# Opening an encoder trunk in two column halves instead of one pass over all columns

## The chip, the core and the metric

The kernel runs on one core of a Trainium2 chip. It is one launch, and its time is the device time of that launch in microseconds (us). The version before took 1982.92 us in the median of three runs (1982.06 to 1983.12). Five engines work side by side, each in the order of its own queue: TensorE (PE) multiplies matrices, VectorE (DVE) and ScalarE (ACT) work element by element, GpSimd (POOL) does a few odd jobs, and SyncE (SP) issues the transfers between HBM and SBUF. A matrix product needs its left operand in the array first; the profile lists this weight load as PEld.

## The reference

Two layers of an encoder are computed on a sequence of 1024 tokens with 1024 channels. This case is about how the first layer begins:

```python
cond = jax.nn.silu(c)                                  # c: (1, 1024)
mod = cond @ ada_w[0] + ada_b[0]                       # ada_w[0]: (1024, 3072)
shift, scale, gate = jnp.split(mod[:, None, :], 3, axis=-1)
h = rmsnorm(x, norm_w[0]) * (1 + scale) + shift
...
proj = h @ w_in                                        # w_in: (1024, 6176)
qkv, z, b, a = jnp.split(proj, [...], axis=-1)         # b and a: 16 columns each
qkv = jax.nn.silu(causal_depthwise_conv(qkv, conv_w))
...
beta = jax.nn.sigmoid(b)
g = -jnp.exp(A_log) * jax.nn.softplus(a + dt_bias)     # per token and head
o = gated_delta_rule(q, k, v, g, beta)                 # cumulative sums of g, a triangular solve
...                                                    # per chunk, a chain of states over chunks
```

Shift and scale are two vectors of 1024 numbers, each a product of the vector `cond` with 4 MB of weights. Nothing of `h` can be computed before they are there. The gates `b` and `a` are 32 more columns of the same projection, and everything behind them (the decay `exp(g)` between tokens of a chunk, the triangular solve, the chain of states) needs them. The second layer is softmax attention with a forget gate; then a final norm follows.

## The kernel before, in words

The first layer works on two halves of 512 tokens. In each it goes through eight groups of heads; a group needs one tile of keys (k), one of queries (q), two of values (v) and two of the output gate (z). A tile is a product of 128 output columns with 512 tokens over eight blocks of 128 channels. Each block takes three matmuls, because the float32 operands are split into a high and a low part (`ht_h`, `ht_l` for the modulated input, `whi`, `wlo` for the weights): high by high, low by high, high by low (`mm3`, line 337). A tile is thus 24 matmuls of 128x512, here called products.

**What sets the order.** The order on TensorE is written by a planner, the class `Flow` (lines 108 to 183). It adds up an assumed cost of each matmul (lines 121 to 128) and switches between generators: a generator that yields a number is left alone until that much assumed time has passed. The projections (`proj_all`, line 802) are the filler of lowest rank, and the gates, the preparation of a group (`prepk`, `prepv`), the triangular solve (`invert_blocks`, `invert_merge`) and the chain of states (`chain`) are put between them at the due times of the constants at the top (`Y_GA`, `LAT` and so on). On the other engines and on SP's queue a list scheduler of the framework sets the order. No engine runs an instruction ahead of one that stands before it in its queue, apart from weight loads on TensorE.

**The opening** (`start_norm`, line 550). Four tiles of x are loaded, normed and transposed into eight blocks `xsT` (tiles named `k`, `q`, `ktok`, 128 channels x 512 tokens each). Shift and scale then come one after the other, each over all 1024 columns (loop of line 570, n = 0 and 1): eight loads of 512 KB, of which VectorE sums the first seven into `acc` (a tile `d2`, lines 577 and 579; `KPE` = 7), and TensorE adds up the 128 rows of `acc` and of the eighth load by matmuls with one column (`ones`, `cond`, line 584). VectorE adds the bias (line 596: `scol` is the shift, `gcol` the scale). Then all eight blocks are modulated: ScalarE writes `ht_h` (line 605) and, for odd blocks, the unrounded value (line 607); VectorE does that for even blocks (line 609) and subtracts for `ht_l` (line 615). The products for the gates take the modulated block as the left operand and 32 columns `wba` as the right one, in unsplit float32 (line 611: 8 blocks x 4 = 32 matmuls of 128x32). Only then the projections begin.

**The gates** (`gates`, line 703). A row of small VectorE operations on 128x64 turns the products into log decays (lines 707 to 718, `g_tmp`), then comes `yield Y_GA` (14000), the cumulative sums on TensorE (lines 722 and 723), four transposes (line 739), a copy by ScalarE (`rows`, line 741), a store to DRAM (`g_d`, line 745), and only with `g_d` there may a group be prepared (line 850). `decay` (line 878) reads two rows of `g_d` back, broadcast to all partitions (`gb`, one buffer), masks them on GpSimd (line 886) and takes eight exponentials on ScalarE (line 897). In `prepk` the keys are transposed, squared and summed on ScalarE (line 943, `sqt`) and copied (line 947); in `prepv` the values are transposed on TensorE (`tr<-ident,vt`) into the two banks `tr`.

**Where the filler ends.** `vt`, the buffer of the value tiles, exists once: the values of group 1 are not projected before those of group 0 are transposed (line 826). So there are 144 products (k, q, v, v of group 0, k and q of group 1) that can run ahead of the gates, and no more.

The next half's x is read early by `next_norm` (line 646): after the gates' cumulative sums two tiles `nx` are loaded, squared by ScalarE (`nh`, line 310) and normed.

## Time and profile before

| | |
|---|---|
| median of three runs | 1982.92 us (1982.06 to 1983.12) |
| the profiled execution | 1981.06 us, its span 1979.3 us, mean granted TensorE clock 0.966 |
| busy share of the span | PE 93%, DVE 67%, ACT 52%, POOL 19% |
| read from HBM, written | 223.15 MB, 81.67 MB |

The profile names an instruction by its line, its engine and the tiles that it writes and reads (`mm<-ht_h,whi`). Times in a timeline row are the start in us from the span's start and the duration; `x3` says that three like instructions are merged in the row; square brackets name idle time of the engine ahead of the row and what ended it. A float32 matmul that isn't split counts as two records. Busy time of TensorE hides its clock: the granted clock has a column of its own.

### The profile page before, as it was taken

What the parts mean: (1) busy time and instruction counts of PE and PEld (TensorE: products, weight loads), DVE (VectorE), ACT (ScalarE), POOL (GpSimd) and SP (SyncE); (2) the same over time, 40 slices, a digit from 0 to 9 for tenths busy, and PEclk for the clock granted to TensorE, in tenths of its full rate; (3) what the DMA queues carried; (4) which work ended last, traced back from release to release, by engine and by line L of the source; (5) the groups of instructions that cost most, each with busy time, mean ns of one, the idle gap of its engine ahead of it and who ended that gap; (6) DMA issues with size and microseconds to landing.
All of it is one profiled execution on the core that took longest, in us unless ns stands there. A gap on an engine that the chain in (4) does not pass through costs nothing.

```text
span 1979.3 us, 35876 instructions
## 1 busy us (share of the span) xinstructions
PE 1838.8 (93%) x12892; PEld 1536.0 (78%) x12892; DVE 1334.9 (67%) x3321; ACT 1030.6 (52%) x2672; POOL 375.2 (19%) x402
## 2 busy tenths in 40 slices
PE   4989989999898999999999889999999999999898
PEld 4868777777786777787777667788988889889676
DVE  6577877888776777776655676456656656656764
ACT  4455656665554445555544444256556655655631
POOL 2010101111111010100010243332232232231322
PEclk6889999999998999999999999999999999999999
DMA  7477556766665564554389985021111120211523
GB/s 265 165 232 245 182 179 198 251 219 225 206 194 170 166 198 146 181 170 137 96 291 311 349 311 201 13 64 49 44 60 38 49 65 27 59 54 49 166 90 96
DMA packets 222874, 307.18 MB, mean 155 GB/s; under 512 B 100396, under 2 KB 136876, under 8 KB 222696
## 3 DMA queue, kind: packets, MB, share of 16 engines
q1 hardware_dynamic: 222696, 304.88, 47.2%
q8 instruction: 102, 1.67, 0.3%
q14 instruction: 76, 0.62, 0.1%
HBM read 223.15 MB, written 81.67 MB: 154 GB/s over the span
## 4 chain that ended last, share of the span: by engine, by line
PE 60%; DVE 15%; DMA 14%; ACT 4%; issue 3%; SPq 3%; POOL 2%; DVEq 0%; POOLq 0%; ACTq 0%
PE mm L132 38%; PE lg L132 5%; PE oT L132 3%; PE pt L136 3%; DMA nx<-in_ada_w_dram 3%; PE su L132 3%; PE tr L136 3%; PE ch L132 2%; DVE wlo L331 2%; DMA lb<-d 1%; PE co L132 1%; DMA lr<-lb 1%; DMA ohi<-og_d 1%; DVE cv_y L792 1%; DVE d L929 1%
## 5 line engine op out<-in xcount | busy, mean ns | idle before, releaser
L132 PE MATMUL mm<-ht_h,whi 128*128 128x512 f32 x768 | 346.2, 451 | 0.2 <-ACT cv_y L784 0.2
L132 PE MATMUL mm<-ht_l,whi 128*128 128x512 f32 x768 | 308.3, 401 | 0.9 <-POOL ht_l L331 0.8
L132 PE MATMUL mm<-ht_h,wlo 128*128 128x512 f32 x768 | 308.6, 402 | 0.0
L132 PE MATMUL mm<-whi,h_h 128*128 128x384 f32 x512 | 186.3, 364 | 0.9 <-DVE kn L1487 0.9
L132 PEld LDWEIGHTS mm<-ht_h,wlo 128*128 128x128 f32 x768 | 148.8, 194 | 34.5
L132 PE MATMUL mm<-whi,h_l 128*128 128x384 f32 x512 | 172.4, 337 | 0.0
L132 PEld LDWEIGHTS mm<-ht_h,whi 128*128 128x128 f32 x768 | 149.9, 195 | 28.6 <-issue 1.7
L132 PE MATMUL mm<-wlo,h_h 128*128 128x384 f32 x512 | 172.1, 336 | 0.0
L132 PEld LDWEIGHTS mm<-ht_l,whi 128*128 128x128 f32 x768 | 149.9, 195 | 26.6 <-POOL ht_l L331 2.0
L1638 DVE TENSOR_TENSOR ptl<-pt,pth 128x512 fp32r<-128x512 f32 x192 | 106.3, 555 | 91.5 <-ACT pth L1637 89.6
L1637 ACT CAST pth<-pt 128x512 fp32r<-128x512 f32 x192 | 91.1, 476 | 138.8 <-PE pt L136 138.0
L792 DVE SCALAR_TENSOR_TENSOR cv_y<-cv_t,conv_h,cv_y 128x512 f32<-128x512 f32 x192 | 143.1, 745 | 16.6 <-ACT cv_y L784 14.4
L331 DVE TENSOR_TENSOR wlo<-ht_h,whi 128x512 fp32r<-128x512 f32 x124 | 97.5, 826 | 47.0 <-ACT whi L328 45.4
L1602 ACT ACTIVATE lg<-lg,mx 128x896 f32<-128x896 f32 (+7 forms) x128 | 99.5, 777 | 53.1 <-DVE mx L1594 47.3
L1481 POOL TENSOR_TENSOR rs<-ss,mhalf 128x4 f32<-128x4 f32 x64 | 64.5, 1007 | 330.6 <-DVE ss L1479 326.2
L328 ACT CAST whi<-ht_h 128x512 fp32r<-128x512 f32 x124 | 70.7, 618 | 89.8 <-DMA ht_h<-in_wa_o_dram 40.1
L132 PE MATMUL mm<-h_h,whi 128*128 128x512 f32 x240 | 99.9, 416 | 0.7 <-DVE wlo L1737 0.3
L132 PEld LDWEIGHTS mm<-whi,h_h 128*128 128x128 f32 x512 | 97.3, 190 | 3.5 <-ACT v L1483 1.2
L132 PEld LDWEIGHTS mm<-wlo,h_h 128*128 128x128 f32 x512 | 96.8, 189 | 2.0
L136 PE MATMUL pt<-ident,lg 128*128 128x128 f32 (+1 forms) x584 | 95.6, 272 | 2.2 <-ACT lg L1602 2.2
L132 PEld LDWEIGHTS mm<-whi,h_l 128*128 128x128 f32 x512 | 96.1, 188 | 0.0
L132 PE MATMUL mm<-h_h,wlo 128*128 128x512 f32 x240 | 94.3, 393 | 0.0
(373 smaller groups left out, 4505.0 us busy)
## 6 DMA issues: line engine op xcount, KB each, us to landing
ht_h<-in_wa_o_dram SPq DMA_DIRECT2D x62, 512.0 KB, 5.6
wc<-whi SPq DMA_DIRECT2D x45, 512.0 KB, 4.3
wc<-wlo SPq DMA_DIRECT2D x45, 512.0 KB, 4.8
wlo<-wc SPq DMA_DIRECT2D x45, 512.0 KB, 4.4
whi<-wc SPq DMA_DIRECT2D x45, 512.0 KB, 3.9
wlo<-in_wa_c_dram SPq DMA_DIRECT2D x35, 512.0 KB, 4.2
nx<-in_ada_w_dram SPq DMA_DIRECT2D x64, 256.0 KB, 4.8
wraw<-in_wb_dram SPq DMA_DIRECT2D x56, 256.0 KB, 2.7
```

The costliest lines, as they stand in the source:

```text
L132: self.nc.tensor.matmul(out, lhsT, rhs, start=start, stop=stop)
L136: self.nc.tensor.transpose(out, src, ident)
L328: nc.scalar.copy(hi, src)
L331: (lo_eng or nc.gpsimd).tensor_tensor(lo, src, hi.bitcast(F32), op=ALU.subtract)
L792: nc.vector.scalar_tensor_tensor(y, raw[:, j : j + HALF], w[:, j : j + 1], y, op0=ALU.mult, op1=ALU.add)
L929: nc.vector.scalar_tensor_tensor(lm[:, u], mq[:, c * P : (c + 1) * P], wn[:, c, j : j + 1], t["d2"][:, u], op0=ALU.mult, op1=ALU.mult,)
L1481: nc.gpsimd.tensor_tensor(rs, ss, mhalf[:, 0:4], op=ALU.pow)
L1602: nc.scalar.activation(lg, lg, AF.Exp, scale=-1.0, bias=mx[:, hh : hh + 1], accum_out=sums[:, tt : tt + 1],)
L1637: nc.scalar.copy(ph_[:, cs], pp[:, cs])
L1638: nc.vector.tensor_tensor(pl_[:, cs], pp[:, cs], ph_[:, cs].bitcast(F32), op=ALU.subtract)
```

## The change

- Shift and scale are no longer computed one after the other over all columns, but together, first for columns 0 to 511 and then for 512 to 1023 (`ada_load`, `ada_sum`). A load is still 512 KB, but each of its rows is now two runs of 2 KB from two places, where it was one run of 4 KB. The small tensors `bcol`, `norm_c`, `wba` and the first weights stand between the two halves, and the sums go to a bank `su`.
- After the first half the blocks 0 to 3 are modulated, and three tiles (`NPRE`, the first three of `proj_all`) begin with their products of those four blocks, in banks `mm`, `mm` and `co`. The first tile goes on with blocks 4 to 7 after the second half, the second with two of them; `proj_tile` finishes the tiles from the list `pre`.
- The gates are now a product with `wba`, split into high and low, as the left operand and 512 tokens as the right one (`gate_mm`, 3 matmuls of 32x512 per block, 24 in all). ScalarE copies the result, four transposes bring it into the form that it had before.
- `Y_GA0` (9000) takes the place of `Y_GA` (14000) for the first half's gates, `LAT0` (33000) that of `LAT` (40000) for the triangular solves of its groups 0 and 1. Both are due times of the planner. Two other lines keep a solve's wait for its banks from being starved (`kept`).

```diff
@@ start_norm: shift and scale @@
-            for n in range(2):
-                ps = banks[n]
-                acc = at([P, D], "d2", 3)
+            def ada_load(c0):
+                acc = at([P, 2, HALF], "d2", 3)
+                ws = []
                 for k in range(KT):
-                    w = at([P, D], *wtag())
-                    nc.sync.dma_start(w, ada_w[0, k * P : (k + 1) * P, n * D : n * D + D])
+                    w = at([P, 2, HALF], *wtag())
+                    nc.sync.dma_start(
+                        w, ada_w[0, k * P : (k + 1) * P, 0 : 2 * D].rearrange("p (n f) -> p n f", n=2)[
+                            :, :, c0 * HALF : c0 * HALF + HALF
+                        ],
+                    )
...
+            def ada_sum(c0, ws):
+                ps = yield from pst("su", 2)
+                for i, (w, c) in enumerate(ws):
+                    for j in range(KT):
+                        n, jj = divmod(j, 4)
+                        mm(
+                            ps[:, j : j + 1], w[:, n, jj * P : (jj + 1) * P], c,
+                            start=i == 0 and j == 0, stop=i == len(ws) - 1 and j == KT - 1,
+                        )
+                cs = slice(4 * c0, 4 * c0 + 4)
+                nc.vector.tensor_tensor(gcol[0][:, cs], ps[:, 4:8], bcol[:, 1, cs], op=ALU.add)
...
@@ start_norm: modulation, gates and first products @@
-                for t in range(CPH):
-                    mm(
-                        pc[:, t * 32 : t * 32 + 32], xk[:, t * P : (t + 1) * P], wba[:, k],
-                        start=k == 0 and t == 0, stop=k == KT - 1 and t == CPH - 1,
-                    )
...
+            split(wbh, wbl, wba, lo_eng=nc.vector)
+            for _ in range(NPRE):
+                wload()
+            half(2 * NPRE)
+            yield from ada_sum(0, ws)
+            ws = ada_load(1)
...
+            def gate_mm(k):
+                mm3(pc[0:32], wbh[:, k], wbl[:, k], ht_h[:, k], ht_l[:, k], k == 0, k == KT - 1)
+
+            def pre_mm(i, k):
+                hi, lo, _ = pws[i]
+                mm3(banks[i], hi[:, k], lo[:, k], ht_h[:, k], ht_l[:, k], k == 0, k == KT - 1)
+
+            for k in range(KT):
+                if k == 4:
+                    yield from ada_sum(1, ws)
+                modulate(k)
+                if k < 4:
+                    for i in range(NPRE):
+                        pre_mm(i, k)
+                    gate_mm(k)
+                else:
+                    gate_mm(k)
+                    pre_mm(0, k)
+            rows = at([P, HALF + 3], "cv_t", 2)[0:32, 0:HALF]
+            nc.scalar.copy(rows, pc[0:32])
...
+            pre_mm(1, 4)
+            pre_mm(1, 5)
...
+                tr_(pg[:, t * 32 : t * 32 + 32], rows[:, t * P : (t + 1) * P], ident[0:32, 0:32])
...
-            yield Y_GA
+            yield (Y_GA0, Y_GA)[h]
...
-            t["end"] = max(flow.t + Y_R2, t0 + LAT)
+            t["end"] = max(flow.t + Y_R2, t0 + (LAT if t["h"] or t["g"] > 1 else LAT0))
```

What this does to the queues is shown at three places. First TensorE, from the sums of shift and scale on. Before, both sums (`mm_267`, `mm_268`, the second in two rows) come first, then the gates, then the first tile:

```order
L132 MATMUL mm_267<-ones_69,d2_270 128x1 x8
L132 MATMUL mm_267<-cond_84,og_292 128x1 x8
L132 MATMUL mm_268<-ones_69,d2_328 128x1 x8
L132 MATMUL mm_268<-cond_84,zg_350 128x1 x8
L132 MATMUL tr_370<-wba_114,k_151 128x32 x4
L132 MATMUL tr_370<-wba_114,k_152 128x32 x4
```

After the first sum the changed kernel has the products of block 0 of three tiles (`mm_368`, `mm_369`, `co_370`), then those of the gates (`tr_367`; `vn` are the halves of `wba`):

```order
L136 MATMUL su_323<-cond_84,og_292 128x1 x8
L136 MATMUL mm_368<-ht_h_149,whi_299 128x512
L136 MATMUL mm_368<-ht_l_150,whi_299 128x512
L136 MATMUL mm_368<-ht_h_149,wlo_301 128x512
L136 MATMUL mm_369<-ht_h_149,whi_307 128x512
L136 MATMUL mm_369<-ht_l_150,whi_307 128x512
L136 MATMUL mm_369<-ht_h_149,wlo_309 128x512
L136 MATMUL co_370<-ht_h_149,whi_315 128x512
L136 MATMUL co_370<-ht_l_150,whi_315 128x512
L136 MATMUL co_370<-ht_h_149,wlo_317 128x512
L136 MATMUL tr_367<-ht_h_149,vn_268 32x512
```

The twelve matmuls of a block repeat for blocks 1 to 3, and only behind these 48 stands the second sum, `su_431`. Then follow three matmuls of the gates and three of the first tile for each of the blocks 4 to 7, six of the second tile, and the four transposes. Ahead of the gates' cumulative sums stand 96 products (before: 69), and ahead of the transposes of group 0's values 144 in both. The solves of groups 0 and 1 stand behind 270 and 339 products (before: 300 and 369); from group 2 to group 6 they stand within 12 products of their old places, later within 36.

Second VectorE, between the two sums. Before, the adds of the second one (`d2_328`, line 579) stand together, with a weight tile's split ahead of the last:

```order
L579 SCALAR_TENSOR_TENSOR d2_328<-og_335,cond_84,d2_328 128x1024
L579 SCALAR_TENSOR_TENSOR d2_328<-zg_338,cond_84,d2_328 128x1024
L579 SCALAR_TENSOR_TENSOR d2_328<-gb_341,cond_84,d2_328 128x1024
L579 SCALAR_TENSOR_TENSOR d2_328<-d1_344,cond_84,d2_328 128x1024
L331 TENSOR_TENSOR wlo_325<-wlo_324,whi_323 128x512 x2
L579 SCALAR_TENSOR_TENSOR d2_328<-og_347,cond_84,d2_328 128x1024
```

In the changed kernel the same adds (`d2_343`, line 591) have the modulation of blocks 0 to 3 between them (lines 622 and 623), and the splits of the second and third weights (`wlo_309`, `wlo_317`) stand behind most of them:

```order
L591 SCALAR_TENSOR_TENSOR d2_343<-zg_353,cond_84,d2_343 128x1024
L623 TENSOR_TENSOR ht_l_150<-k_151,ht_h_149 128x512
L622 TENSOR_SCALAR k_153<-k_153,gcol0_88,scol0_90 128x512
L591 SCALAR_TENSOR_TENSOR d2_343<-gb_356,cond_84,d2_343 128x1024
L623 TENSOR_TENSOR ht_l_150<-k_152,ht_h_149 128x512
L623 TENSOR_TENSOR ht_l_150<-k_153,ht_h_149 128x512
L623 TENSOR_TENSOR ht_l_150<-q_154,ht_h_149 128x512
L591 SCALAR_TENSOR_TENSOR d2_343<-d1_359,cond_84,d2_343 128x1024
L339 TENSOR_TENSOR wlo_309<-wlo_308,whi_307 128x512 x2
L591 SCALAR_TENSOR_TENSOR d2_343<-og_362,cond_84,d2_343 128x1024
L339 TENSOR_TENSOR wlo_317<-wlo_316,whi_315 128x512 x2
```

Between the first sum's columns and the first half of `wlo_317` VectorE has five adds, two modulations, four subtractions and three half splits.

Third VectorE at the gates. Before, the operations on `g_tmp` stand together, and the convolution of the first tile (`cv_y`) follows them:

```order
L323 SCALAR_TENSOR_TENSOR g_tmp<-g_tmp 128x64 x6
L324 SCALAR_TENSOR_TENSOR g_tmp<-g_tmp 128x64
L717 SCALAR_TENSOR_TENSOR g_tmp<-g_tmp 128x64
L718 TENSOR_TENSOR g_tmp<-g_tmp,neg_a 128x64
L331 TENSOR_TENSOR wlo<-wlo,whi 128x512 x2
L792 SCALAR_TENSOR_TENSOR cv_y<-cv_t,conv_h,cv_y 128x512 x3
L799 SCALAR_TENSOR_TENSOR k<-cv_t,cv_y 128x512
```

In the changed kernel they are spread between the convolutions of the first four tiles; these are the last rows of that stretch:

```order
L855 SCALAR_TENSOR_TENSOR cv_y_649<-cv_t_648,conv_h_110,cv_y_649 128x512
L331 SCALAR_TENSOR_TENSOR g_tmp_530<-g_tmp_530 128x64
L332 SCALAR_TENSOR_TENSOR g_tmp_530<-g_tmp_530 128x64
L774 SCALAR_TENSOR_TENSOR g_tmp_530<-g_tmp_530 128x64
L862 SCALAR_TENSOR_TENSOR vt_579<-cv_t_648,cv_y_649 128x512
L775 TENSOR_TENSOR g_tmp_530<-g_tmp_530,neg_a_113 128x64
L782 COPY g_gc_662<-tr_659 128x128
```

From the first operation of the gates (line 764) to the last (line 775), with which the cumulative sums can start, VectorE now has 12 convolution steps, 4 closing products of a tile (line 862), 6 half splits of weights and the gates' own operations. On ScalarE two rows change place: the copy of the gates' rows (line 798) stands behind the squares of `nx` (line 318), which need that tile's load, and the last of the four squares and the copy of group 0's keys stand behind the exponentials of the second group's decay (`d2_843`).

75 lines of the change are left out of this document (47 added, 28 removed).

## The prediction

> **What bounds the kernel now.** I read the busy times by stretches first (columns: busy us and records of PE, PEld, DVE, ACT, POOL; then the granted TensorE clock, DMA share, GB/s).
>
> ```profile
> 40.00:60.00 20.00, 14.90 (x70) 14.68 (x70) 8.06 (x14) 8.57 (x12) 0.00 (x0) 0.50 0.00 0
> 60.00:80.00 20.00, 20.00 (x79) 16.72 (x79) 11.93 (x29) 5.69 (x12) 0.72 (x3) 0.81 0.38 134
> 100.00:120.00 20.00, 14.11 (x70) 11.90 (x69) 11.55 (x36) 14.80 (x52) 5.36 (x7) 0.83 0.72 227
> 220.00:240.00 20.00, 16.40 (x93) 14.28 (x92) 19.61 (x60) 13.19 (x44) 3.96 (x5) 0.87 0.61 211
> 240.00:260.00 20.00, 14.41 (x103) 11.76 (x105) 15.38 (x67) 10.12 (x32) 1.30 (x2) 0.93 0.50 120
> ```
>
> TensorE is the bound nearly everywhere, but not at the start: until 60 us its clock is at half and it does nothing of the projections; between 100 and 120 it idles for 6 us. The timeline of the opening shows why.
>
> ```profile
> 27.68 0.17 DVE L596 TENSOR_TENSOR scol<-mm,bcol 128x8 f32<-128x8 f32 x1 [0.38 <-PE mm L132]
> 43.34 0.17 DVE L596 TENSOR_TENSOR gcol<-mm,bcol 128x8 f32<-128x8 f32 x1 [5.23 <-PE mm L132]
> 43.81 2.22 ACT L605 ACTIVATE ht_h<-k,scol,gcol 128x512 fp32r<-128x512 f32 x3 [6.50 <-DVE gcol L598]
> 50.32 3.63 PE L132 MATMUL tr<-wba,k 128*128 128x32 f32 x16 [3.15 <-ACT k L607]
> 62.29 0.77 PE L132 MATMUL mm<-ht_h,whi 128*128 128x512 f32 x1
> 62.51 0.23 DVE L707 TENSOR_TENSOR g_tmp<-tr,dt_b 128x64 f32<-128x64 f32 x1 [9.41 <-PE tr L132]
> 67.31 0.23 DVE L718 TENSOR_TENSOR g_tmp<-g_tmp,neg_a 128x64 f32<-128x64 f32 x1
> 67.53 0.39 PE L132 MATMUL mm<-ht_h,whi 128*128 128x512 f32 x1
> 80.46 0.33 PE L132 MATMUL tr<-g_tmp,triu 128*128 128x64 f32 x2
> ```
>
> The shift is there at 27.68, the scale at 43.34; then the gates' products run until 62.29, and there both the projections and the gates' operations begin. The 12 products up to 67.53 take 0.44 us each, the 57 up to 80.46 take 0.227: the clock comes up only under them. What limits the next 45 us is the last fence of this part, the way from the gates' cumulative sums (80.46) to the values' transposes.
>
> ```profile
> 82.36 0.24 DVE L654 COPY nx<-g_ngc 128x8 f32<-128x8 f32 x2
> 84.96 1.28 SPq L745 DMA_DIRECT2D g_d<-cv_t  x1
> 100.92 1.10 POOL L886 TENSOR_SCALAR_AFFINE_SELECT d<-gb 128x1024 f32<-128x1024 f32 x1 [2.92 <-PE su L132]
> 102.05 2.44 ACT L897 ACTIVATE d<-d,g_ngc 128x128 f32<-128x128 f32 x8 [2.10 <-POOL d L886]
> 107.61 1.11 PE L136 MATMUL tr<-ident,vt 128*128 128x128 f32 x4 [5.89 <-ACT vtok L964]
> 108.38 0.78 PE L132 MATMUL mm<-ht_h,whi 128*128 128x512 f32 x1
> 111.92 0.40 PE L132 MATMUL mm<-ht_h,wlo 128*128 128x512 f32 x1
> ```
>
> By 102 TensorE has done all 144 products that may run ahead of the gates; it waits 5.89 us and resumes at 108.38, at half clock until 111.92. So what counts is when this chain ends, and not how many of the 144 products were done early: **resume at 108.38** is the mark against which I set the change. From it on both kernels have the same work left.
>
> **The change, step by step** (on the clock of the profiled execution). The prices:
>
> ```profile
> 29.07 1.28 DVE L579 SCALAR_TENSOR_TENSOR d<-zg,cond,d 128x1024 f32<-128x1024 f32 x1
> 36.82 1.29 DVE L331 TENSOR_TENSOR wlo<-wlo,whi 128x512 fp32r<-128x512 f32 x2 [0.56 <-ACT whi L328]
> 44.65 0.55 DVE L609 TENSOR_SCALAR k<-k,gcol,scol 128x512 f32<-128x512 f32 x1 [0.94 <-ACT ht_h L605]
> 45.23 0.69 DVE L615 TENSOR_TENSOR ht_l<-k,ht_h 128x512 fp32r<-128x512 f32 x1
> 49.46 0.80 ACT L607 ACTIVATE k<-k,scol,gcol 128x512 f32<-128x512 f32 x1
> 526.97 0.95 PE L132 MATMUL mm<-ones,nh 128*128 128x1 f32 x8
> 5.00:19.00 14.00, 7.70 (x32) 5.98 (x32) 10.09 (x14) 10.68 (x41) 6.07 (x11) 1.00 1.03 401
> 1000.00:1020.00 20.00, 17.05 (x90) 13.08 (x89) 9.32 (x18) 8.83 (x21) 0.00 (x0) 1.00 1.02 365
> ```
>
> 1. *First columns.* The adds and the sum of the first half are as many as before, so they end as at 27.68. Three small operations in place of one cost 0.4 us. The loads now run in pieces of 2 KB. With rows of 4 KB the engines moved 401 GB/s, in the output projection, with rows of 1 KB among them, 365 at the same share: at most 10% of eight loads of 1.3 us, 1.0 us. I take 0.4, the middle being nearer to 4 KB. The Trainium skill (DMA: Bandwidth & Descriptors, Specifications) states that a transfer of 512 B or more runs at line rate. By it the term is zero and the sum 0.4 us lower; no run here shows pieces of 2 KB alone. Columns at 28.6.
>
> 2. *VectorE up to the third weight.* Five adds (1.3), two modulations (0.55), four subtractions (0.69), three half splits (0.65) are 6.5 + 1.1 + 2.8 + 2.0 = 12.3 us in one queue: 40.9. Until then TensorE has 9 of its 48 products, since `wlo_309` and `wlo_317` are split behind the adds. The adds themselves end at 40 (before: 36.3), hidden under the products.
>
> 3. *The other 39 of the 48*: 12 at 0.44, then 27 at 0.227, 11.4 us: 52.3. All at full clock it would be 8.9, all at half 17.
>
> 4. *Second sum.* 32 records; 43.34 less the 36.3 at which the adds ended, 7.0 us, at half clock, 0.1 us each at full clock (the row at 526.97): 3.2 to 7.0. I take 3.5, since 28 products just ran: 55.8. Here is the price of the new order: the second sum was done at 43.3.
>
> 5. *Second half.* Columns 0.5 us; four `ht_h` at 0.71, one unrounded block 0.8, one subtraction 0.69 until block 5 is there: 60.7. TensorE has six products meanwhile and cools down. Then 17 products: 8 at half clock in 3.5 us, as from 108.38 to 111.92, and 9 at 0.227: 66.2. Six more, 1.4, and four transposes, 0.6, stand ahead of VectorE's first operation on the gates: **68.2, where it was 62.51**. The 12 us of float32 gate products (50.32 to 62.29) are gone, but 54 products and a late second half stand in their place. The row of 111.92 is what the Trainium skill says (TensorE: Matmul & The Clock Gate, The HAM clock gate): an idle window of about 3.4 us halves the clock, a busy one restores it. By it the first heating of step 3 would be 3.4 us too, and the sum 0.8 us lower; the rows at 62.29 and 67.53 show 5.2.
>
> 6. *The gates' operations.* The rows for these:
>
> ```profile
> 72.48 2.33 DVE L792 SCALAR_TENSOR_TENSOR cv_y<-cv_t,conv_h,cv_y 128x512 f32<-128x512 f32 x3 [0.30 <-ACT cv_y L784]
> 75.56 0.69 DVE L799 SCALAR_TENSOR_TENSOR k<-cv_t,cv_y 128x512 f32<-128x512 f32 x1 [0.76 <-ACT cv_t L796]
> ```
>
> They took 5.0 us in one piece (62.51 to 67.54). Now 12 convolution steps (0.78, 9.3 us), four closing products (2.8) and six half splits (3.9) stand among them in the same queue: 21.0 us, ending at 89.2. The 42 products that TensorE has ahead of the cumulative sums are through at 77.7, so it waits 11 us there. **Cumulative sums at 89.2, before 80.46: 8.7 later.**
>
> 7. *From there to the resume* it was 27.9 us. The row copy now waits for `nx`.
>
> ```profile
> 1.23 1.37 SPq L555 DMA_DIRECT2D vtok<-in_x_dram  x3
> 5.10 1.06 ACT L310 ACTIVATE nx<-vtok 128x1024 f32<-128x1024 f32 x1 [2.48 <-DMA vtok<-in_x_dram]
> 98.05 0.58 ACT L947 COPY ktok<-tr 128x512 f32<-128x512 f32 x1
> 102.05 0.32 SPq L881 DMA_DIRECT2D gb<-g_d  x1
> 107.08 1.09 POOL L886 TENSOR_SCALAR_AFFINE_SELECT d<-gb 128x1024 f32<-128x1024 f32 x1
> lb<-d SPq DMA_DIRECT2D x8, 32.0 KB, 2.3
> ```
>
> With nothing queued ahead 512 KB took 3.9 us (1.23 to 5.10) and its squares 1.25: with 1.9 for the copies at 82.36, the copy starts 7.1 us after the sums, not 3.9: +3.2. `g_d` and `gb` took 16.0 together (84.96 to 100.92), with weights and x queued ahead; now little is: 2.3 for the store (as `lb`, the same size) and 5.0 for the read (102.05 to 107.08): -8.6. From the mask to the resume it was 7.5. Now the keys' last square and copy stand behind the second group's exponentials: mask 1.1, second read 5.0, mask 1.1, exponentials 2.4, square and copy 1.0, a tanh and four squares 2.4, transposes 0.8, 13.8: +6.3. Net +0.9, between -3.5 (each transfer a third shorter) and +5 (reads at 7 us).
>
> Resume at 89.2 + 27.9 + 0.9 = 118.0: **9.6 us later.**
>
> 8. *Behind it.* The solves of groups 0 and 1 stand 30 products (6.8 us) nearer.
>
> ```profile
> L1148 DVE STREAM_TRANSPOSE tmat<-rmat x8: 432/436/441, 143.4 to 169.1; 32x256 f32<-32x256 f32 x8
> L132 PE MATMUL su<-tmat,d x160: 177/191/267, 157.5 to 200.9; 16*32 16x16 f32 x64, 32*32 32x32 f32 x64, 64*64 64x64 f32 x32
> ```
>
> The first solve's input was ready at about 145 and used at 157.5: 12 us to spare, which cover the 6.8. I take nothing for it, with 0 to 4 us if the input comes later too. From group 2 on the order is nearly the old one and TensorE the bound, so what is lost at the mark stays lost.
>
> The sum is 1981.06 + 9.6 = 1990.7 us for an execution like the profiled one. That one is 1.9 below the median of the three runs, so I predict **1992.5**. Its own range, from the ends above (gates' start 66 to 71, their stretch 20.4 to 23, step 7 24.5 to 32; not all at once), is 1986 to 1999.
>
> **Rivals.**
> - *The head start pays.* At 67.6 the changed kernel has 54 products done, the one before had them at 67.53 + 42 x 0.227 = 77.1: 9.5 us. If the gates' chain were not what TensorE waits for, all of it would stay: 1973.4. For it speaks that TensorE is busy all through 60 to 100, against it the 5.89 us wait at 107.61. It decides if VectorE reaches the end of the gates' stretch by 71, 18 us sooner than I have it. Chance 0.11.
> - *Short ends, and chains that start sooner.* All of steps 3 to 7 at their short ends put the resume at 109.6, 1.2 later; and the waits of 220 to 260, 9.2 us of idle TensorE by the rows above, go, because the first chains of states stand 30 products further ahead of the filler: 1982.9 + 1.2 - 9.2 = 1974.9. Chance 0.15.
> - *Given back.* The mark is 9.6 late, but those 9.2 us go: 1983.3. VectorE at 19.61 of 20 between 220 and 240 speaks against, since its work is the same. Chance 0.11.
> - *Worse.* TensorE is at half clock through steps 3 and 4 (+8.5) or the solves wait (+4): +14 to +18, 1997 to 2001. Chance 0.18.
>
> That the change does not do what it says is excluded by its order. My forecast keeps 0.45.
>
> **The numbers.** A difference of 0.2%, 4 us, is about what can be told from no change here. Slower by more: forecast, *worse* and a bit of *given back*, 0.64; within: 0.10; faster: 0.26. The range 1975 to 2001 leaves out the first rival, the lower part of the second and the upper end of *worse*, 0.2 in all.
>
> **What would show it.** Right: the second sum's matmuls begin past 50; the gates' first VectorE operation past 66; the cumulative sums with an idle TensorE of about 10 us ahead of them, near 89; the first product behind the values' transposes near 118. Wrong: a resume before 108, or a resume near 118 with an unchanged end.

## The result, and the profile after

| | before | changed |
|---|---|---|
| median | 1983.02 us (4 runs, 1982.06 to 1985.96) | 2013.78 us (4 runs, 2010.19 to 2020.31) |
| ratio, 95% interval | | 1.0162, 1.014 to 1.0185 |
| the profiled execution | 1981.06 us, span 1979.3 us | 2010.19 us, span 2008.0 us |
| mean granted TensorE clock | 0.966 | 0.963 |
| busy share of PE, DVE, ACT, POOL | 93%, 67%, 52%, 19% | 92%, 66%, 51%, 18% |

The change costs 31 us, three times what was forecast, and beyond the upper end of the range. The opening itself went nearly as worked out. These are the rows of the changed kernel's timeline that answer to the steps (start, duration, engine, line, what; in square brackets the idle time ahead and what ended it):

```profile
24.59 3.58 PE L136 MATMUL su<-cond,og 128*128 128x1 f32 x16 [0.58 <-DMA og<-in_ada_w_dram]
29.13 0.15 DVE L608 TENSOR_TENSOR gcol<-su,bcol 128x4 f32<-128x4 f32 x1
40.64 0.79 PE L136 MATMUL co<-ht_h,wlo 128*128 128x512 f32 x1 [0.31 <-DVE wlo L339]
...
52.01 1.84 PE L136 MATMUL su<-ones,d 128*128 128x1 f32 x16
55.81 0.16 DVE L608 TENSOR_TENSOR gcol<-su,bcol 128x4 f32<-128x4 f32 x1 [14.62 <-PE su L136]
67.38 0.22 DVE L764 TENSOR_TENSOR g_tmp<-tr,dt_b 128x64 f32<-128x64 f32 x1
85.71 0.22 DVE L775 TENSOR_TENSOR g_tmp<-g_tmp,neg_a 128x64 f32<-128x64 f32 x1
86.08 0.66 PE L136 MATMUL tr<-g_tmp,triu 128*128 128x64 f32 x2 [8.98 <-POOL cv_t L850]
...
100.16 1.10 POOL L949 TENSOR_SCALAR_AFFINE_SELECT d<-gb 128x1024 f32<-128x1024 f32 x1 [4.02 <-DMA gb<-g_d]
110.13 0.57 ACT L1010 COPY ktok<-tr 128x512 f32<-128x512 f32 x1
110.75 1.11 PE L140 MATMUL tr<-ident,vt 128*128 128x128 f32 x4 [8.32 <-ACT ktok L1010]
112.73 1.12 PE L140 MATMUL tr<-ident,vt 128*128 128x128 f32 x4 [0.87 <-ACT sqt L1006]
```

The second sum begins at 52.01, the gates' row on VectorE at 67.38 and ends at 85.93; TensorE stands idle for 8.98 us ahead of the cumulative sums, and the products resume at about 113.5 us, where it was 108.38. That is 5 us late, not 9.6. So 24 of the 29 us by which the two profiled executions differ are lost behind the mark, where the prediction had put nothing.

To see where, I put a price on each matmul of both traces (the median time to the next matmul, where that one had not waited), summed the prices from the end backwards, and asked for each kernel at what time it has the same TensorE work left as the kernel before. The differences in us, positive when later (the columns behind the first are experiments told below; each is one profiled execution, which can lie 5 us off the median of its kernel, as in runs 7 and 16):

```
time in the  changed  old due  due times prefetch both    one piece  opening,   gates   one tile
kernel before         times    alone     as bef.  undone  in changed one piece  first   deeper
                      (2)      (3)       (5)      (7)     (18)       (14)       (15)    (17)
 120           +5.0    +1.7     -0.8      +6.1     +4.2    -2.7       -9.0       -8.7    -2.0
 220           +5.1    +2.7     -1.9      +5.0     +4.4    -6.9       -7.7       -7.8    -1.1
 280           -4.3    +3.2     -7.2      +0.8     -1.3   -11.4       -6.2       -6.2    -1.1
 520           -0.4    -3.1    -10.9      +2.1     +2.4    -6.3       -6.3       -5.4    -1.5
 560          +11.5    +5.1     -8.8      +3.0     +3.4    +4.8       -5.2       -0.2    +6.9
1000           +8.5    +9.4     -4.9      +6.6     +1.2    +4.9       -0.5      +13.3    +7.5
1100          +13.2    +8.3     -5.1      +9.4     +1.9   +10.6       -0.2      +11.4    +8.5
1200          +23.1    +6.3     +9.8     +24.7     +2.5   +19.2       -3.0      +10.0   +10.5
1960          +28.7    +8.7    +11.1     +26.5    +10.4   +21.3       -0.7      +13.5   +12.3
```

The changed kernel is 5 us late at the mark, *ahead* by 4 us at 280, level at 520, and then loses 12 us at 520 to 560 and 10 us between 1100 and 1200. Of the rest, 3 us come back between 560 and 1000, 5 are lost between 1000 and 1100, and some 5 in small pieces behind 1200.

The gain at 220 to 280 is seen in the busy times by stretch (columns as in the prediction): TensorE is busy for 36.2 of 40 us, before for 30.8.

```profile
220.00:240.00 20.00, 20.00 (x118) 17.49 (x117) 19.52 (x62) 13.23 (x42) 4.96 (x6) 1.00 0.58 200
240.00:260.00 20.00, 16.20 (x196) 12.78 (x195) 17.24 (x52) 10.74 (x34) 0.47 (x2) 0.91 0.87 266
...
530.00:550.00 20.00, 11.63 (x166) 8.48 (x164) 10.24 (x15) 9.01 (x23) 4.44 (x4) 0.74 0.54 161
```

The last row is the first loss: 11.63 us of TensorE in 20, at a granted clock of 0.74. There the second half of the tokens begins. Its normed input is read back from DRAM (`wlo<-h_d`, line 753), ScalarE rounds it to `ht_h`, and the products go on. The timeline of the changed kernel there, from SP's queue to TensorE:

```profile
526.96 9.52 SPq L278 DMA_DIRECT2D nx<-in_ada_w_dram  x5
536.53 0.44 SPq L753 DMA_DIRECT2D wlo<-h_d  x1
...
540.96 1.14 ACT L336 CAST ht_h<-wlo 128x512 fp32r<-128x512 f32 x2 [3.91 <-DMA wlo<-h_d]
...
541.63 0.79 PE L136 MATMUL mm<-ht_h,whi 128*128 128x512 f32 x1 [7.55 <-ACT ht_h L336]
```

And in the kernel before, where the same product starts at 530.63 without a wait:

```profile
530.00:550.00 20.00, 18.29 (x234) 13.71 (x233) 17.08 (x30) 12.97 (x36) 5.97 (x7) 1.00 0.83 282
...
525.38 0.91 SPq L696 DMA_DIRECT2D wlo<-h_d  x2
...
529.11 1.14 ACT L328 CAST ht_h<-wlo 128x512 fp32r<-128x512 f32 x2 [2.63 <-DMA wlo<-h_d]
```

The read is 11 us later, so TensorE waits 7.55 us. The second loss lies in the output projection, which reads `ohi`, `olo` and weights at a DMA share of 0.8 to 1.0. The end of its first half in the changed kernel:

```profile
1125.88 0.42 SPq L1389 DMA_DIRECT2D v<-x_d  x1
1126.35 0.42 SPq L342 DMA_DIRECT2D kn<-in_wb_dram  x1
1127.31 0.32 SPq L1389 DMA_DIRECT2D v<-x_d  x1
1127.67 0.96 SPq L342 DMA_DIRECT2D kn<-in_wb_dram  x1
1128.73 0.59 SPq L443 DMA_DIRECT2D ohi<-og_d  x1
...
1135.56 0.77 PE L136 MATMUL mm<-whi,ohi 128*128 128x512 f32 x1 [4.82 <-DMA ohi<-og_d]
```

and in the kernel before:

```profile
1113.41 0.32 SPq L435 DMA_DIRECT2D ohi<-og_d  x1
...
1114.77 0.32 SPq L1326 DMA_DIRECT2D v<-x_d  x1
1115.14 0.42 SPq L334 DMA_DIRECT2D kn<-in_wb_dram  x1
...
1122.83 0.77 PE L132 MATMUL mm<-whi,yh 128*128 128x512 f32 x1 [3.11 <-DMA yh<-og_d]
```

Four loads of layer 2 (twice 512 KB, twice 256 KB) stand ahead of the last `ohi`, before they stood behind it. The stretch in the changed kernel, with its GB/s in the last column:

```profile
1120.00:1140.00 20.00, 12.45 (x44) 8.29 (x42) 5.55 (x12) 7.03 (x14) 4.77 (x5) 0.85 0.94 324
```

1.5 MB at 324 GB/s would take 4.7 us (an estimate from this row), and TensorE waits 4.82. But the kernel before waits 3.11 us at its next load, `yh`, so these two waits don't make up the 10 us; what the order of these loads costs is left to runs 6 to 8. From its first to its last product, taken from the trace, the whole projection lasts 249.7 us, before 236.0.

### The profile page after: what moved, and what is told of

Its sections match the earlier page's. It is cut to its first block, busy times and chain, and to the rows that moved or that the text cites. A ratio compares the mean times of both kernels' runs of the same rounds, so it can differ in the third digit from the quotient of the medians.

```text
span 2008.0 us, 35824 instructions
## 1 busy us (share of the span) xinstructions
PE 1839.9 (92%) x12856; PEld 1527.5 (76%) x12856; DVE 1331.4 (66%) x3325; ACT 1033.7 (51%) x2674; POOL 365.0 (18%) x402
## 4 chain that ended last, share of the span: by engine, by line
PE 58%; DMA 17%; DVE 14%; ACT 4%; issue 3%; SPq 3%; POOL 1%; DVEq 0%; POOLq 0%; ACTq 0%
PE mm L136 36%; PE lg L136 5%; DMA nx<-in_ada_w_dram 3%; PE pt L140 3%; PE oT L136 3%; PE su L136 3%; PE ch L136 3%; PE tr L140 2%; DMA ohi<-og_d 2%; DVE wlo L339 2%; PE co L136 2%; DVE cv_y L855 1%; DMA ht_h<-in_wa_o_dram 1%; DMA lr<-lb 1%; DMA wraw<-in_wb_dram 1%
## 5 line engine op out<-in xcount | busy, mean ns | idle before, releaser
L136 PEld LDWEIGHTS mm<-ht_l,whi 128*128 128x128 f32 x760 | 148.3, 195 | 28.2 <-DVE ht_l L623 2.3
L339 DVE TENSOR_TENSOR wlo<-ht_h,whi 128x512 fp32r<-128x512 f32 x122 | 91.1, 783 | 53.3 <-ACT whi L336 49.1
```

Source lines behind the costliest of these rows:

```text
L136: self.nc.tensor.matmul(out, lhsT, rhs, start=start, stop=stop)
L339: (lo_eng or nc.gpsimd).tensor_tensor(lo, src, hi.bitcast(F32), op=ALU.subtract)
```

## The experiments

Times are medians in us, ratios against the kernel before on the same chip with their 95% intervals (the changed kernel: 1.0162). Where one differs from its neighbour by less than about 0.3% it tells little: the intervals are that wide.

**1. The reads ahead of the modulation loads.** The first theory was SP's order, in which eight of those loads stand right ahead of the read. Here they must wait for the first read's tile (`where["hf"]`).

```diff
@@ ada_all @@
-            for l, cl in strips:
+            for m, (l, cl) in enumerate(strips):
+                if m == 3:
+                    yield from hold(lambda: "hf" in where)
+                    for _ in range(2):
+                        nc.vector.tensor_copy(al([P, KT], "nx", 2), where["hf"])
```

> The changed kernel, with one edit far from the opening: the loads of layer 2's modulation weights (`nx<-in_ada_w_dram`) from the 25th on may only be issued once the first read of the second half's input (`wlo<-h_d`) has landed. In SP's queue of the changed kernel 34 of them stand ahead of those reads, in the kernel before 26, here 24. *Theory A (two far queues)*: the opening itself costs 5 us at the resume of the products and has given them back by 255 us; the 29 us arise from SP's order at 522 to 536 us (20 us) and from VectorE's order at 1204 to 1221 us (12 us). Then this edit takes 14 to 20 us off, 1994 to 2000; the VectorE order at the second place stands like that of the kernel before here too, and if that counts the time is 1982 to 1988. *Rival B (carried loss)*: what the opening lost is only waited out at 541 us, and would be waited out at the next place otherwise: 2008 to 2016.

Measured: 2015.28, ratio 1.0157 (1.0133 to 1.018). Theory A fell. The modulation loads were gone from there, and still:

```profile
535.87 2.11 SPq L753 DMA_DIRECT2D wlo<-h_d  x2
...
539.46 1.14 ACT L336 CAST ht_h<-wlo 128x512 fp32r<-128x512 f32 x2 [1.72 <-DMA wlo<-h_d]
...
540.13 0.80 PE L136 MATMUL mm<-ht_h,whi 128*128 128x512 f32 x1 [4.30 <-ACT ht_h L336]
```

The read is now issued at 535.87 because a product ended at 535.85, the first half's last: it waited for its buffer `wlo`. The order of the queue was a symptom.

**2. Opening alone, planner as before.**

```diff
-Y_GA0 = 9000
-LAT0 = 33000
+Y_GA0 = 14000
+LAT0 = 40000
@@ Flow.bank @@
-        while key in self.kept:
-            yield 150
```

> The changed kernel with the planner as before: Y_GA0 = 14000, LAT0 = 40000 and without the two lines of `kept`; the opening in two halves alone. Its SP queue has 27 of the loads ahead of the second half's reads (before 26, changed 34). *Theory A*: the far loss at 522 to 557 us is gone, the opening's few us stay: 1980 to 1995. *Rival B (carried loss)*: the opening is what costs, so about the changed kernel's time or more, since the later due times hold the gates back too: 2008 to 2020. *Rival C (the due times cost)*: the new due times are badly set and are the loss, so 1975 to 1985 here.

Measured: 1993.23, ratio 1.0053 (1.0031 to 1.0074), by A's number; but A's reason had fallen, so it says only that opening and due times each do harm.

**3. Due times alone, opening as before.** The three edits of the planner in the old kernel.

> The kernel before with only the planner's part of the change: Y_GA0 = 9000, LAT0 = 33000, `kept`. The opening is the old one. 28 loads stand ahead of the second half's first read and 33 ahead of the last (before 26 and 28). *Theory A*: no loss of its own, 1978 to 1992. *Rival C (the due times cost)*: 2000 to 2012. *Rival B*: as before, 1981 to 1986.

Measured: 1995.09, ratio 1.0062 (1.004 to 1.0085), between A and C. The trace shows more than the time: it is 11 us ahead at 520, and loses 15 us between 1100 and 1200 (third column above), where the changed kernel loses 10. Its projection takes 249.0 us; with the old due times (run 2) it takes 232.9.

**4. The second norm raised in priority.**

```diff
-            scaled(xt, n2jk[t])
+            with tc.high_priority(offset=1000):
+                scaled(xt, n2jk[t])
```

> The changed kernel with the small operations of the second norm (sum, reciprocal root, scaling of `v`) of the last four token tiles raised in the scheduler's priority. In VectorE's queue the scaling of the second tile comes two operations sooner, and the transposed blocks of the next one follow it directly. Nothing is changed at 522 to 557 us. *Theory A*: of the 12 us lost at 1204 to 1221 us some part returns, 2002 to 2012. *Rival B*: no difference, 2011 to 2016.

Measured: 2014.23, ratio 1.014 (1.0097 to 1.0184): no difference to be told, and its projection takes 249.2 us. Raising these operations returns nothing of the 13.7 us by which the projection is longer.

**5. One weight tile less ahead.** In the changed kernel the three tiles begun early each issue a new weight load, so the line of loaded weights is longer by one tile from then on. A tile takes two of the five `wlo` buffers, in a ring, and the reads of `h_d` use the same ring.

```diff
@@ proj_tile @@
                 (hi, lo, key), ps, k0 = pre.pop(0)
-                wload()
+                if len(pre) < NPRE - 1:
+                    wload()
```

> The first run showed that putting the modulation loads behind the reads of the second half's input saves nothing: there the reads wait for a buffer `wlo` that comes free only with the last product of the first half (read issued at 535.87, freed at 535.85). *Theory D (one weight tile too many)*: each of the three tiles begun early issues a new weight load when it is finished, so from then on one more weight tile is loaded ahead; it takes two more of the five `wlo` buffers, and the four reads stand behind it in the ring: 51 weight loads ahead of them, in the kernel before 50. All three kernels with the new opening wait there for `ht_h` (7.6, 4.3 and 4.4 us), the two with the old one do not. This kernel leaves out one of the three loads, so 50 stand ahead. Expected by D: reads issued before the first half's last product, no wait for `ht_h`, 8 to 12 us less, 2001 to 2006. *Rival B (carried loss)*: the time is waited out elsewhere, 2010 to 2016.

Measured: 2007.7, ratio 1.0129 (1.01 to 1.0158), 0.33% or 6.5 us less. The mechanism is as D has it: the first two reads go out after 1131 and 1139 of the first half's 1152 products, where the changed kernel had started all 1152, and no product waits for `ht_h`. The loss at 520 to 560 is 0.9 us instead of 11.9. The time fell by less, since this execution is 2.5 us later at 520 and loses 15 us in the projection.

**6. Layer 2's loads behind the last loads of the first half's projection.**

```diff
@@ preload; the same ahead of the first two reads v<-x_d @@
             raw = bt([P, 2, 512], "kn")
+            yield from hold(lambda: "lasto" in where)
+            for k in range(2):
+                nc.vector.tensor_copy(raw[:, k, 0:KT], where["lasto"][:, 0:KT].bitcast(F32))
```

> *Theory E (next phase too early)*: in both kernels with the new due times the output projection takes 249 to 250 us from its first to its last product, in the two with the old ones 233 to 236. The chain of layer 1 ends after 216 instead of 246 of its products, and at its end buffers for layer 2 come free: eight weight loads (`kn`) and two reads of x are then queued ahead of the last loads of the first half's projection, at a DMA share of 0.95 to 1. Here they may only be issued once the last of these loads has landed; everything else is as in the changed kernel. Expected by E: the projection back at 234 to 240 us, 9 to 14 us less, 2000 to 2005. *Rival F (volume)*: the projection is bound by its own loads, and what is taken from one place is waited out at the next: 2010 to 2016.

Measured: 2014.34, ratio 1.017 (1.0138 to 1.0202). By the time alone E falls. The projection became shorter, 242.1 us, but the wait for `ht_h` is 8.28 us here and this execution already 20 us late at 560. So the run did not decide between E and F.

**7. Both edits.**

> The edits of the two kernels ahead of this one together, in the changed kernel. By D and E the two sum up: 2013.8 less 17 to 26, 1988 to 1997. By D alone 2001 to 2006, by E alone 2000 to 2005, by B and F 2010 to 2016.

Measured: 1996.7, ratio 1.0075 (1.0048 to 1.0101): D and E together. The projection takes 235.7 us, as before the change; 0.54% less than with the prefetch alone.

**8. Due times alone, with the loads of run 6 held back.**

> The kernel before with the new due times alone (1995 as measured) and the loads of layer 2 held back as in the run on the next phase. By E it loses the 13 us of its longer projection and keeps the 4 to 5 us by which it is ahead at 1000 us: 1978 to 1986. By F 1991 to 1998.

Measured: 1982.27, ratio 1.0012 (0.9994 to 1.0029); 1995 without the hold. E holds: the projection takes 237.0 instead of 249.0 us.

**9. Without `kept`.** By the order, the chain of layer 1 ends after 216 products of the projection in the changed kernel and in run 3, after 246 in the kernel before; leaving out the two lines of `Flow.bank` shown in run 2 puts it back to 246.

> The changed kernel without the two lines of `kept` (a generator that wants a bank is no longer turned away while a solve collects its four banks); opening and due times stay. By the order the chain of layer 1 then ends after 246 products of the output projection again, as in the kernel before, and the loads of layer 2 stand behind 128 of its loads, not 126. *Theory E, sharpened (it is `kept` that brings the next phase forward)*: the projection takes 233 to 238 us, not 249.7, and the time is 2013.8 less 9 to 14: 2000 to 2005; the loss at the second half's first products (theory D) stays. *Rival G (the due times bring it forward)*: 2010 to 2016.

Measured: 2004.98, ratio 1.0122 (1.0102 to 1.0142), as E has it: the projection takes 233.7 us. In the traces the first two solves stand behind 300 and 369 products again, as in the kernel before, where the changed kernel has 270 and 339, and the first chain of states starts behind 369 instead of 339. So it is `kept` that moves the solves and chains ahead, both here and in the projection, and it is not only harm. Without it the waits at 240 to 280 are there again (TensorE busy 30.2 of 40 us), and the execution is 8.4 us late at 280, where the changed kernel is 4.3 ahead:

```profile
240.00:260.00 20.00, 14.66 (x80) 12.01 (x79) 18.73 (x70) 9.12 (x34) 1.44 (x3) 0.91 0.47 159
260.00:280.00 20.00, 15.49 (x218) 12.36 (x216) 12.75 (x49) 9.68 (x36) 0.62 (x3) 0.83 0.44 111
```

**10. Without `kept`, and one weight tile less.**

> The changed kernel without `kept` and with one weight load less ahead (the edit of the run on the prefetch): both losses taken back at their causes, the opening and the due times stay. By D and E: as the run with both edits, 1988 to 1997 (that gave 1996.7), and what the opening costs at the mark, 5 us, is what is left: 1986 to 1992. If the due times bring their 4 to 8 us ahead of the chains as in the run of due times alone: 1978 to 1986. Rival B: over 2000.

Measured: 2001.86, ratio 1.0111 (1.0085 to 1.0137): later than expected by 10 us. Rival B's number, though both losses are gone from the trace (projection 235.1 us). It is 8.0 us late at 280, where run 7, which has `kept`, is 1.3 ahead: that much of what `kept` had brought is gone. At the end the two differ by 0.36%, with overlapping intervals.

**11. Y_GA0 and LAT0 alone in the old kernel.**

> The kernel before with Y_GA0 = 9000 and LAT0 = 33000 alone, no `kept`. By E nothing is lost in the output projection and the 4 to 8 us that the earlier solves bring remain: 1973 to 1982. Rival G: 1991 to 1998, as with `kept`.

Measured: 1989.87, ratio 1.0041 (1.0021 to 1.0061). Expected was a gain, and it is a loss of 8 us. The projection is as short as before (235.5 us), but the earlier due times alone bring 3 us at 280 and lose them by 500. They leave the first two solves behind 300 and 369 products, as in the kernel before; in run 3 these stand behind 270 and 339. So most of the gain of run 3 came from `kept` (with these due times; `kept` alone was not run).

**12. The gates' row in one piece** (on run 10). The convolutions of the first two tiles get their three zero columns as the gates' result times zero, so they wait for it. A `yield 0` behind `start_norm` came with this edit, here and in runs 14, 16 and 18.

```diff
@@ proj_conv @@
-                nc.gpsimd.memset(raw[:, 0:3], 0.0)
+                if done["conv"] < 2:
+                    nc.gpsimd.tensor_scalar(raw[:, 0:3], where["gr"][:, 0, 0:3], 0.0, None, op0=ALU.mult)
+                else:
+                    nc.gpsimd.memset(raw[:, 0:3], 0.0)
...
@@ proj_all @@
                         yield from start_norm()
+                        yield 0
```

> The kernel of the second run of this batch, and in it the convolutions of the first two tiles wait for the gates' last VectorE operation (their three zero columns are written as that result times zero), so VectorE does the gates' row in one piece of about 6 us instead of 18.5. This is for steps 6 and 7 of the prediction. *Theory H (the chain from the gates sets the resume)*: cumulative sums at 76 to 80 us instead of 86, resume of the products 6 to 9 us sooner, and 4 to 8 us off the whole time. *Rival I*: the resume is sooner, but the solves and chains that follow are not, and less than 2 us of it is left at the end.

Measured: 1995.24, ratio 1.0076 (1.0048 to 1.0104), 0.35% less than run 10, with overlapping intervals. The resume is 7 us sooner. It speaks for H, weakly.

**13. Opening alone, one weight tile less** (run 2 with the edit of run 5).

> The opening in two halves with the planner as before (Y_GA, LAT, no `kept`) and one weight load less ahead, as in the kernel before. What is left of the change is the opening itself. *Theory J (the opening itself costs little, theory D is its main loss)*: the 10 us of the run with the old due times less 5 to 8: 1985 to 1989. *Rival K (the opening itself costs)*: less than 3 us returns, 1990 to 1994; the rest is the late gates and what follows them.

Measured: 1996.57, ratio 1.0073 (1.0049 to 1.0097). J falls: the wait for `ht_h` is gone (4.36 us in run 2), and the time is not shorter, but later than either had it. K's reading, that the opening itself costs, is what the next run tests.

**14. Run 13 with the gates' row in one piece.**

> As the kernel ahead of this one, and the convolutions of the first two tiles wait for the gates' last VectorE operation. The gates' row is one piece again; the cumulative sums still stand behind 120 products. *Theory H (the chain from the gates sets the time)*: the resume 5 to 8 us sooner and 4 to 8 us off the time of the kernel ahead. *Rival I (the solves behind the mark have another bound)*: less than 2 us.

Measured: 1981.66, ratio 0.9999 (0.9982 to 1.0015): 0.74% or 15 us less than run 13, twice what H expected. The opening in two halves is then no slower and no faster than the old one.

**15. Gates first.** As run 13, but no tile is begun early, and two weight tiles are loaded ahead instead of three.

```diff
@@ start_norm @@
             for k in range(KT):
                 if k == 4:
                     yield from ada_sum(1, ws)
                 modulate(k)
-                if k < 4:
-                    for i in range(NPRE):
-                        pre_mm(i, k)
-                    gate_mm(k)
-                else:
-                    gate_mm(k)
-                    pre_mm(0, k)
+                gate_mm(k)
```

> The opening in two halves with the planner as before, but no product of a tile is begun early: sum of the first half, modulation and gate products of blocks 0 to 3, second sum, the same for blocks 4 to 7, gates, then the tiles. Weights are loaded ahead as in the kernel before. So the second sum is not behind 48 products, and VectorE has the gates' row without convolutions among it. By the prediction's own steps (the chain behind the gates sets the resume, products done early do not count) the gates' first operation comes at 51 to 54 us in place of 62.5, the sums after 69 products at about 70 (before 80.5), the resume near 98 to 101 (before 108.4). *Theory H*: that stays to the end, 1971 to 1977. *Rival I*: the resume is that early, but less than 3 us of it is left at the end: 1979 to 1985.

Measured: 1989.75, ratio 1.0039 (1.0023 to 1.0054): slower than either had it. Its opening is nearly as expected:

```profile
54.64 0.23 DVE L742 TENSOR_TENSOR g_tmp<-tr,dt_b 128x64 f32<-128x64 f32 x1 [4.31 <-PE tr L140]
59.43 0.22 DVE L753 TENSOR_TENSOR g_tmp<-g_tmp,neg_a 128x64 f32<-128x64 f32 x1
...
71.97 0.33 PE L136 MATMUL tr<-g_tmp,triu 128*128 128x64 f32 x2
...
99.27 1.11 PE L140 MATMUL tr<-ident,vt 128*128 128x128 f32 x4 [6.04 <-ACT vtok L1005]
```

The row takes 5 us and the resume comes 8.7 us sooner than before, just as in run 14 (-8.7 and -9.0 at 120), where 48 products stand ahead of the second sum and here none. So products done early do not count at the mark. But 7 us are lost at 600 to 640, where TensorE waits 5.28 and 2.78 us for VectorE in two solves, and more behind 900. I did not find out why VectorE's order there is worse than in run 14.

**16. Run 7 with the gates' row in one piece.**

> The changed kernel with both losses taken back (prefetch as before, next phase held back; 1996.7 as measured) and the gates' row in one piece. *Theory H*: 1988 to 1992. *Rival I*: 1994 to 1998.

Measured: 1983.75, ratio 1.0004 (0.9987 to 1.0021): 0.71% or 14 us less than run 7. With three causes taken back, the changed kernel is level with the one before.

**17. The kernel before, one weight tile deeper.**

```diff
@@ proj_tile @@
                 if k == 1:
                     wload()
+                    if "deep" not in where:
+                        where["deep"] = 1
+                        wload()
```

> The kernel before with nothing changed but one weight tile more loaded ahead (a third load is issued once, during the first tile). 51 weight loads then stand ahead of the reads of the second half's input, as in the changed kernel. *Theory D*: the reads are issued only at the first half's last product, TensorE waits for `ht_h` there by 4 to 8 us, and the time is 4 to 10 us longer, 1986 to 1993. *Rival*: the wait is there, but given back later, less than 3 us: 1980 to 1986.

Measured: 1991.55, ratio 1.0045 (1.0029 to 1.006). D by itself, in the old kernel, costs 8.9 us. All 1152 products had started when the first read went out:

```profile
528.85 0.43 SPq L696 DMA_DIRECT2D wlo<-h_d  x1
532.84 0.38 SPq L696 DMA_DIRECT2D wlo<-h_d  x1
...
533.36 0.50 PE L132 MATMUL mm<-ht_h,whi 128*128 128x512 f32 x1 [3.88 <-ACT ht_h L328]
```

**18. The changed kernel, gates' row in one piece.**

> The changed kernel with the gates' row in one piece (convolutions of the first two tiles behind it) and nothing else. With both losses taken back one piece gave 13 us (1996.7 to 1983.75), in the opening alone 15 (1996.57 to 1981.66), without `kept` 7. *Theory H (the causes add up)*: 1997 to 2004. *Rival (the far waits absorb it)*: 2008 to 2016.

Measured: 2002.52, ratio 1.0105 (1.0084 to 1.0126): 0.57% or 11 us less than the changed kernel. H holds here too. Its row and what follows:

```profile
66.87 0.22 DVE L764 TENSOR_TENSOR g_tmp<-tr,dt_b 128x64 f32<-128x64 f32 x1
73.32 0.23 DVE L775 TENSOR_TENSOR g_tmp<-g_tmp,neg_a 128x64 f32<-128x64 f32 x1
...
76.42 0.33 PE L136 MATMUL tr<-g_tmp,triu 128*128 128x64 f32 x2
97.68 0.66 PE L140 MATMUL tr<-ident,vt 128*128 128x128 f32 x4 [1.97 <-ACT ktok L1016]
```

6.7 us instead of 18.5, and the values' transposes begin at 97.68, not at 110.75.

**The sum.** Three things were each taken away from the changed kernel or a relative of it, and the time fell: the gates' row spread out among the convolutions (11 us in the changed kernel, 14 behind the other two edits), the weight tile too many (6.5, and 8.9 when added to the old kernel), and `kept` with layer 2's loads in the output projection (0.54% from run 5 to run 7, 10.7 us; 9.9 from run 3 to run 8). 11.3 + 6.5 + 10.7 are 28.5 of the 31 us, and without all three (run 16) the time is that of the kernel before. This is not a full account, for three reasons.

- The intervals leave some 6 us to each, and such prices don't always show by themselves: in runs 6 and 13 one edit removed its wait and none of the time.
- A gates' row in one piece does more than restore. The products resume at 105.43 us in run 18, 105.14 in run 16 and 99.51 in run 14, where the kernel before has 108.38. So it also makes up for losses behind the mark that no run has located: run 13, with a row as long as that of the changed kernel (66.34 to 87.73), is level at 120 us and 15.6 late at the end, and run 14 loses 8 us between the same two points.
- The due times `Y_GA0` and `LAT0` cost something too. With them and without `kept`, run 10 is 0.38% slower than run 13 (overlapping intervals), run 9 is 0.69% slower than run 2, and run 11 is 0.41% slower than the kernel before. No run takes them back and leaves `kept` in place.

## Why the prediction was wrong, point by point

1. *First columns* at 28.6: 29.13. The last load arrived 0.58 us after TensorE was ready for it. The Trainium skill's rule that pieces of 512 B or more run at line rate (DMA: Bandwidth & Descriptors, Specifications) would have had 28.2; the trace speaks rather for a small cost, but no run separates the pieces from the order of the loads.
2. *Third weight split* at 40.9: 40.64. Right.
3. *The other 39 products* end at 52.3: 52.01. Right in sum. The clock came up sooner than I took it, as the rows show, the time from one to the next being 0.42 up to 45.07 and 0.23 from 45.33 on:

```profile
44.65 0.61 PE L136 MATMUL mm<-ht_h,wlo 128*128 128x512 f32 x1
45.07 0.42 PE L136 MATMUL co<-ht_h,whi 128*128 128x512 f32 x1
45.33 0.39 PE L136 MATMUL co<-ht_l,whi 128*128 128x512 f32 x1
45.56 0.39 PE L136 MATMUL co<-ht_h,wlo 128*128 128x512 f32 x1
```

   From 40.64, behind the last pause, that is 4.4 us: between the 3.4 us window of the Trainium skill (TensorE: Matmul & The Clock Gate, The HAM clock gate) and my 5.2.

4. *Second sum* at 55.8: 55.81. Right.
5. *Gates' first operation* at 68.2: 67.38. Right.
6. *The gates' row* takes 21.0 us: 18.5, and TensorE waits 8.98 us for it (11 forecast). The mechanism was right and 2.5 us too large. Its worth was not: without the spread (run 18) the products resume 8.1 us sooner, and the time is 11 us shorter.
7. *From the sums to the resume* 28.8: 27.4 (86.08 to about 113.5). Its parts came out within 1 us each: the row copy 7.0 us behind the sums (7.1), store and read 6.4 (7.3), mask to resume 13.3 (13.8). So the mark was 5 late, not 9.6. The largest addition, the second group's exponentials (+6.3), was read rightly from the order, but not tied to its cause. In this kernel, with its spread row, it comes with the new due time. The changed kernel has two groups' exponentials on ScalarE ahead of the resume, the kernel before one (102.05):

```profile
101.29 2.44 ACT L960 ACTIVATE d<-d,g_ngc 128x128 f32<-128x128 f32 x8 [4.93 <-POOL d L949]
107.53 2.45 ACT L960 ACTIVATE d<-d,g_ngc 128x128 f32<-128x128 f32 x8
```

   Run 13 has the old due time, a row that is as long, and one group's exponentials ahead:

```profile
87.88 0.66 PE L136 MATMUL tr<-g_tmp,triu 128*128 128x64 f32 x2 [6.38 <-DVE g_tmp L773]
103.42 2.44 ACT L959 ACTIVATE d<-d,g_ngc 128x128 f32<-128x128 f32 x8 [3.28 <-POOL d L948]
107.41 1.11 PE L140 MATMUL tr<-ident,vt 128*128 128x128 f32 x4 [6.55 <-ACT vtok L1026]
```

   Its sums come 1.8 us later than in the changed kernel and its products resume at 108.17, level with the kernel before. Run 10, with the new due times, has two groups ahead and resumes at 113.68.
8. *Behind it.* This step failed: "From group 2 on the order is nearly the old one and TensorE the bound, so what is lost at the mark stays lost", and with it "From it on both kernels have the same work left". Nothing stayed. By 280 us 9 us came back, which was the rival *given back*, with a price of 9.2 that the trace confirms. The reason given for it under *short ends* holds as well: the first chains start behind 339 products instead of 369, and in run 9, where they start behind 369 again, the waits are back. What moves them is `kept`; without it (runs 9 to 11) the new due times leave them where they were. Then 12 us went at 520 to 560 and 10 at 1100 to 1200, through two lines for which the sum had no term: a third `wload()` in `proj_tile`, and `kept`. Both can be read off the order, since 51 weight loads stand ahead of the second half's reads where there were 50, and the chain ends after 216 products of the projection where there were 246. I had followed the order only up to the first solves, and taken a likeness of positions within 36 products for no difference.

The sign was right, but in part by luck: what was lost at the mark was back by 280 us, and of the three things whose removal shortened the time the sum had one, the gates' row. The *short ends* were also added wrongly: by the ends stated for the range, 66 + 20.4 + 24.5, they give 110.9 and not 109.6, and that rival 1976.2; nothing else hangs on it.

Of the core of the working one half held. Products done early do not count at the mark: run 14 has 48 of them ahead of the second sum and run 15 none, and they resume at 99.51 and 100.03. But the gates' sums do not set the resume by a fixed distance, as step 7 took it from the kernel before (27.9 us). From the sums to the resume it is 17.5 us in run 14, 20.3 in run 13, 28.1 in run 15 and 33.1 in run 11. In run 14 the first mask comes at 103.61, after the resume, so there the resume waits for no group's exponentials; TensorE waits 2.72 us for the copy of the gates' rows instead. And in run 11 the sums come 5.8 us sooner than in the kernel before, but two groups' exponentials stand ahead of the resume, and it comes only 0.6 us sooner (107.75).

## What to carry to other kernels

Follow every buffer and queue that an edit touches to the end of the program, not to the end of the stage: a prefetch that is one tile deeper moves the next user of the same ring, however far off. Look at what a latency-bound row of small operations is queued with on its engine; new work that becomes ready beside it can stretch it several times over, here from 5.0 to 18.5 us. And read a planner's side edits, here two lines against starving, as changes of their own: `kept` moved the first solves and the start of a whole phase by 30 products each; the one brought 9 us by 280, the other put the phase's loads into a stretch with a DMA share of 0.94.

## What the runs showed that I had not expected

A resume 9 us sooner need not be worth anything at the end: run 14 is 9.0 us ahead at 120 and 5 us ahead until 900, and level from 1000 on. Between 900 and 1000 its granted clock is low twice: 0.91 from 920 to 940 and 0.83 from 960 to 980, where the kernel before had 1.00 in both (and 0.91 from 900 to 920). Each of these stretches has a wait of TensorE for the chain of states in it, of 2.52 us at 923.77 and 2.27 at 975.21. But the kernel before waits 2.70 us at the like place, 977.25, at a clock of 1.00, so the wait alone does not explain the clock. Run 15, with the same resume, is slower than the kernel before by 0.4%. How much of this comes from the order that the list scheduler happened to give VectorE stays open.
